# Dividing the input by its rms before the projection, and moving projection results and chain copies from VectorE to ScalarE

## The chip, the cores and the metric

The kernel runs on one core of a Trainium2 chip. A core has TensorE (PE in the profile, matmuls; PEld its weight loads), VectorE (DVE), ScalarE (ACT), GpSimd (POOL) and SyncE (SP, whose queue issues the DMAs here). The metric is the device time of one run in microseconds (us). Before the change it is 3194.62 us, the median of three runs from 3189.17 to 3198.58.

## The reference, cut to what matters

One layer of a hybrid decoder trunk over a prompt of 2048 tokens and 8 single-token samples, all in float32, width 1024. The part that the change touches:

```python
h = rmsnorm(x, norm_mix)                      # x / sqrt(mean(x*x)) * w, per token
p = h @ w_in                                  # 1024 -> 3980 columns, one projection for all groups
# group A: gated DeltaNet, chunks of 64 tokens
qkv = silu(causal_conv(p_a, 4 taps));  q, k = l2norm(q), l2norm(k)
v_new = u_i - w_i @ s                         # chunk by chunk, s carried from chunk to chunk
s = s * g_last + k_dec.T @ v_new
# group B: RWKV-7, the same carried state in another form
decay = exp(-exp(w0 + tanh(wd) @ w2)); a = sigmoid(a0 + ad @ a2)
# group C: HGRN2, chunks of 64
x = x + concat(y_a, y_b, y_c) @ w_out
x = x + (silu(h2 @ w_gate) * (h2 @ w_up)) @ w_down      # h2 = rmsnorm(x)
y = rmsnorm(x)
```

The rms of a token is one number per column of `p` in the kernel's transposed layout, so it can be applied to `x` ahead of the product or to `p` behind it.

## The kernel before, in words

Everything is kept transposed: features on the 128 partitions, tokens along the free axis. The tokens are cut into four quarters (`QS`): three of 512 and a last one of 520 (512 prompt tokens and the 8 samples), which is taken as two passes of 260 columns.

A large product is three matmuls for each of 8 slices of the contraction (`mm3`, L377 to L379): weight and input are split into a high and a low part, and high*high, high*low and low*high are added up in one PSUM bank. So one tile of the projection (128 output features by 512 tokens, tile `psp`) is 24 matmuls of 128x512. The pool `pg` has three banks for them. `proj` (L471) makes the 31 tiles of a quarter and multiplies each with the quarter's `rstd` on DVE (L482) on its way to the tile `p`, which a DMA then stores in DRAM (`s_p`). `split_x` (L409) makes the high part of the input on ACT (L417) and the low part on DVE (L418); `xs` has 8 buffers, one for each slice, so a quarter's first split waits until the quarter before has used that slice for the last time. `stats_x` (L426) makes `rstd`: squares on ACT, their sum on DVE, a matmul with ones, and Ln and Exp on ACT (`rsqs`, L290, with a table load at L285). It also makes the 12 columns `pba` of the projection (L447) and multiplies them with `rstd` (L452). For quarters 1 to 3 it runs at the sixth of the eight groups of tiles (`AT` = 5) of the quarter before.

From the stored `p` the mixers work, for each quarter three units of group A (`gdn`), three of B (`rwkv`) and two of C (`hgrn`). A unit of A or B has a first stage (convolution at L827 to L829, or token shift and decay, then triangular inverses) and a second one, a chain over 8 chunks. In each chunk stand three steps of small matmuls, `px`, `pv` and `pS`, with a result on DVE between any two of them: `X` (L900 or L1121), `Z` or `SA` (L906, L1128), and the next `Z` (L913, L1134). The second stages of one A unit and one B unit often run at the same time.

After the projections come, quarter by quarter, the output product (tile `pso`), and the FFN (`pfg`, `pfu`, `pd`); a quarter's end normalisation (`final`, tiles `pny` and `ry`) is done in steps within the next quarter's `out_proj`.

The program's order is made in two steps. `Driver` (L1460) takes turns: each turn advances all live units by one step and then emits as many large products as a rate for the quarter allows. The framework then sorts each engine's instructions by its own planning. Each engine runs its list strictly in that order, so an instruction that waits holds up all behind it on that engine; TensorE's list mixes large products with small matmuls of the mixers.

Of the kernel before, what the change touches and what calls it, by code (L numbers as in the profile page):

```python
# [13 lines left out]
AF = mybir.ActivationFunctionType  # L14
ALU = mybir.AluOpType
# [11 lines left out]
G = 512  # L27
# [3 lines left out]
QS = ((0, 512), (512, 512), (1024, 512), (1536, 520))  # L31
# [60 lines left out]
class Kern:  # L92
# [332 lines left out]

    def stats_x(self, q, load):  # L426

        nc = self.nc
        acc = self.new_acc(f"i{q}")
        if q == 0:  # L430
            nc.sync.dma_start(self.wba, self.io["wba"].rearrange("p (k j) -> p k j", j=32)[:, :, 0:12])
            nc.vector.tensor_tensor(self.wba, self.wba, self.parw("norm_mix")[:, :, None].to_broadcast([128, 8, 12]),
                                    ALU.mult)

        with ExitStack() if q else self.tc.issue_after(self.last.ins):
            for k in range(8):
                self.add_square(acc, load[k], self.cols(q), k == 0, f"i{q}", self.S if q else self.T)
        rstd = self.norm_stats(acc, self.cols(q), f"i{q}", q == 0)

        new = self.S if q else self.T  # L440
        p = new(f"pba{q}")
        for c0, cn in self.cols(q):
            cs = slice(c0, c0 + cn)
            ps = self.bank(f"psb{q}_{c0}")[:, :cn]
            for k in range(8):
                j = 32 * (k % 4)
                nc.tensor.matmul(ps[j:j + 12], lhsT=self.wba[:, k], rhs=load[k][:, cs], start=k < 4, stop=k > 3,  # L447
                                 tile_position=(0, j))
            nc.vector.tensor_copy(p[0:12, cs], ps[0:12])
            for j in (32, 64, 96):  # L450
                nc.vector.tensor_tensor(p[0:12, cs], p[0:12, cs], ps[j:j + 12], ALU.add)
            nc.vector.tensor_tensor(p[0:12, cs], p[0:12, cs], rstd[0:12, cs], ALU.mult)  # L452
        self.ba(q, p)
        return rstd

# [15 lines left out]
    def proj(self, qs, m, xs, rstd, w=None, stats=None, held=()):  # L471

        nc = self.nc
        w = w or held or self.load_w(self.io["w1"][m], ("in", m), qs[0])
        for q in qs:
            t0, n = QS[q]
            p = self.E(f"p{q}_{m}")
            for c0, cn in self.cols(q):
                ps = held[0] if held else self.gemm8(w, xs[q], c0, cn, f"psp{q}_{m}_{c0}")
                if q not in rstd:  # L480
                    rstd[q] = stats()
                nc.vector.tensor_tensor(p[:, c0:c0 + cn], ps, rstd[q][:, c0:c0 + cn], ALU.mult)  # L482

            if q < 3:
                nc.sync.dma_start(self.s_p[q + 1][m, :, 0:HALO], p[:, G - HALO:G])
            else:
                nc.scalar.activation(self.tail[:, m], p[:, G - HALO:G], AF.Copy)
                nc.scalar.activation(self.smp[:, m], p[:, G:G + NS], AF.Copy)
            self.mark = nc.sync.dma_start(self.s_p[q][m, :, HALO:], p[:, :n])
# [263 lines left out]
    def half(self, pair, h, other=False):  # L753

        return self.heads(pair[h], other)(h)
# [40 lines left out]
    def gdn(self, q, u):  # L796

        nc = self.nc
        t0 = QS[q][0]
        nm = f"g{q}{u}"  # L800
# [3 lines left out]
        def first():  # L804
# [18 lines left out]
            for which in (1, 0, 2):  # L823
                pt = self.slice_p(q, T_G + 4 * u + which, 3, f"p_{nm}")
                x = kq2[:, 1 - which] if which < 2 else self.T(f"cv_{nm}")
                wi = 4 * (3 * which + u)
                nc.vector.tensor_scalar(x, pt[:, 3:3 + G], self.par("conv", wi + 3), None, ALU.mult)  # L827
                for j in (2, 1, 0):
                    nc.vector.scalar_tensor_tensor(x, pt[:, j:j + G], self.par("conv", wi + j), x, ALU.mult, ALU.add)  # L829
                yield  # L830
                self.gate(x, x)
                if which < 2:
                    sq = self.T(f"sq_{nm}")
                    nc.scalar.activation(sq, x, AF.Square)
                    sums[which] = self.bsum(f"ss_{nm}", sq), sq
                    made = made or self.mm
                    yield
# [50 lines left out]
        def second():  # L888
            U, Q, kb3, vb3, kd, sg = (box[n] for n in ("U", "Q", "kb", "vb", "kd", "sg"))

            Z = [ch(self.T(f"Z{h}_{nm}")) for h in range(2)]
            st = self.state["g", u]
            for h in range(2):
                nc.vector.tensor_copy(half(Z, h)[:, 0], st[H[h]])
            for c in range(GC):
                px = self.ps(f"px_{nm}")[:, 0:64]
                for h in range(2):
                    nc.tensor.matmul(px[H[h]], lhsT=kb3[H[h], c], rhs=half(Z, h)[:, c], start=True, stop=True)
                X = self.X(f"X_{nm}")
                nc.vector.tensor_tensor(X, px, vb3[:, c], ALU.add)  # L900
                yield
                pv_ = self.ps(f"pv_{nm}")[:, 0:64]
                for h in range(2):
                    nc.tensor.matmul(pv_[H[1 - h]], lhsT=U[H[h], c], rhs=X[H[h]], start=True, stop=True)
                for h in range(2):
                    nc.vector.tensor_copy(half(Z, h, True)[:, c], pv_[H[1 - h]])  # L906
                yield
                pS = self.ps(f"pS_{nm}")[:, 0:64]
                for h in range(2):
                    nc.tensor.matmul(pS[H[h]], lhsT=kd[H[1 - h], c], rhs=half(Z, h, True)[:, c], start=True, stop=True)  # L910
                for h in range(2):
                    to = half(Z, h)[:, c + 1] if c + 1 < GC else st[H[h]]
                    nc.vector.scalar_tensor_tensor(to, half(Z, h)[:, c], sg[H[h], c:c + 1], pS[H[h]],  # L913
                                                   ALU.mult, ALU.add)
                yield
            yield NEXT
            po = self.ps(f"po_{nm}")
            for c in range(GC):
                for h in range(2):
                    nc.tensor.matmul(ch(po)[H[h], c], lhsT=Z[h][:, c], rhs=Q[h][:, c], start=True, stop=True)  # L920
            z = self.slice_p(q, T_G + 4 * u + 3, 0, f"z_{nm}")
            self.gated_norm(po, z, self.gnw2, nm, u, t0)
# [69 lines left out]
    def rwkv(self, q, u, lo):  # L992
# [7 lines left out]
        def first():  # L1000
# [4 lines left out]
            lw, cu = self.T(f"lw_{nm}"), self.T(f"cu_{nm}")  # L1005
            ps = self.ps(f"pw_{nm}")
            nc.tensor.matmul(ps, lhsT=self.w2a2[0:64, us], rhs=wa[0:64], start=True, stop=True)
            self.rwkv_decay(lw, ps, u)
            nc.vector.tensor_tensor_scan(cu, self.reset, lw, 0.0, ALU.mult, ALU.add)
            yield  # L1010

            f = self.sp.tile([128, GC], F32, tag="f", name=f"f_{nm}")
# [12 lines left out]
            nc.scalar.activation(e1, e1, AF.Exp)  # L1025
            nc.scalar.activation(e2, d, AF.Exp)
            nc.scalar.activation(d, d, AF.Exp, scale=-1.0)
            a = self.T(f"a_{nm}")
            ps = self.ps(f"paa_{nm}")
            nc.tensor.matmul(ps, lhsT=self.w2a2[64:128, us], rhs=wa[64:128], start=True, stop=True)  # L1030
            self.rwkv_rate(a, ps, u)
            yield
            k = self.shifted(q, T_R + 3 * u + 1, 3 + u, f"k{nm}")
            kr = self.TT(f"kr_{nm}")
            kk, r, t = kr[:, 0], kr[:, 1], self.T(f"t_{nm}")
# [74 lines left out]
        def second():  # L1110
# [5 lines left out]
            for c in range(GC):  # L1116
                px = self.ps(f"px_{nm}")[:, 0:64]
                for h in range(2):
                    nc.tensor.matmul(px[H[h]], lhsT=W[0][h][:, c], rhs=Z[h][:, c], start=True, stop=True)
                X = self.X(f"X_{nm}")  # L1120
                nc.vector.tensor_copy(X, px)  # L1121
                for h in range(2):
                    nc.vector.scalar_tensor_tensor(KV[H[h], c], half(Z, h)[:, c], f[H[h], c:c + 1], KV[H[h], c],
                                                   ALU.mult, ALU.add)
                yield
                pv_ = self.ps(f"pv_{nm}")[:, 0:64]
                self.pair(lambda p: pv_[p], lambda p: U[p, c], lambda p: X[p])
                nc.vector.tensor_copy(SA[:, c], pv_)  # L1128
                yield
                pS = self.ps(f"pS_{nm}")[:, 0:64]  # L1130
                self.pair(lambda p: pS[p], lambda p: bt[p, c], lambda p: SA[p, c])
                if c + 1 < GC:
                    for h in range(2):
                        nc.vector.tensor_tensor(half(Z, h)[:, c + 1], pS[H[h]], KV[H[h], c], ALU.add)  # L1134
                else:
                    nc.vector.tensor_tensor(st, pS, KV[:, c], ALU.add)
                yield
# [561 lines left out]
```

## Time and profile before

| | |
|---|---|
| median of three runs | 3194.62 us (3189.17 to 3198.58) |
| profiled execution | 3185.85 us, span 3184.1 us |
| PE busy | 3063.0 us (96%), 24812 matmuls |
| DVE busy | 2189.0 us (69%), 5424 instructions |
| ACT busy | 1196.6 us (38%), 2064 instructions |
| granted TensorE clock, mean | 0.985 of full speed |
| HBM traffic | 628.01 MB by DMA, 197 GB/s |

The busy shares are over the whole span. Three stretches differ: up to about 1014 us the projections and the mixers of the first quarters run together, from there to about 2640 us the FFNs and the remaining mixers, and behind that only large products of the last quarters. A matmul's duration in the profile overlaps the next one's, so what a matmul costs is read from start to start, not from its length.

### The profile page before, as it was taken

The page shows a single profiled execution, that of the slowest core. Times are in us where ns is not written, and L with a number is a line of the kernel's source. Part 1 is how long each engine was busy: PE and PEld are TensorE (multiplying, and loading weights), DVE is VectorE, ACT ScalarE, POOL GpSimd, SP SyncE. Part 2 cuts the span into 40 slices and gives each one's busy share as a digit, 9 for nine tenths or more (in the row PEclk, how much of TensorE's full clock was granted, in tenths as well). Part 3 has the DMA queues.
Part 4 walks back from the last instruction along what each step waited for, and adds up shares of the span by engine and source line. Part 5 has one row for each costly group of instructions (what it writes and reads, how often), then busy time and mean ns, then how long its engine had stood idle before and what let it go on. Part 6 is the DMA issues. An engine that isn't in the chain of part 4 may idle for free.

```text
span 3184.1 us, 62691 instructions
## 1 busy us (share of the span) xinstructions
PE 3063.0 (96%) x24812; PEld 2442.2 (77%) x24812; DVE 2189.0 (69%) x5424; ACT 1196.6 (38%) x2064; POOL 12.3 (0%) x41
## 2 busy tenths in 40 slices
PE   7999999999998999999989999999999999999998
PEld 5767767778897677677766777777777777999998
DVE  6783666677768888896978778868877653443334
ACT  5452243245324544543555334445433221221002
POOL 0000000000000000000000000000000000000000
PEclk9999999999999999999999999999999999999999
DMA  8877666657656766677764454557554465755552
GB/s 286 287 244 250 193 182 199 207 168 228 185 164 172 235 229 221 223 221 257 226 219 149 153 163 146 190 165 233 165 162 150 151 216 183 251 170 186 189 182 90
DMA packets 391971, 628.01 MB, mean 197 GB/s; under 512 B 172988, under 2 KB 177340, under 8 KB 391676
## 3 DMA queue, kind: packets, MB, share of 16 engines
q1 hardware_dynamic: 390588, 622.93, 61.4%
q8 instruction: 195, 3.19, 0.4%
q10 hardware_dynamic: 1088, 1.07, 0.1%
q14 instruction: 100, 0.82, 0.1%
HBM read 456.77 MB, written 167.14 MB: 196 GB/s over the span
## 4 chain that ended last, share of the span: by engine, by line
PE 68%; DVE 13%; DMA 11%; ACT 4%; SPq 2%; issue 2%; DVEq 0%; ACTq 0%
PE psp L377 5%; PE psp L379 5%; PE psp L378 5%; PE pfg L378 4%; PE pfg L377 4%; PE pfg L379 4%; PE pfu L377 4%; PE pfu L378 4%; PE pfu L379 4%; PE pd L377 4%; PE pd L379 4%; PE pd L378 4%; PE pso L377 1%; PE pso L378 1%; PE pso L379 1%
## 5 line engine op out<-in xcount | busy, mean ns | idle before, releaser
L377 PE MATMUL psp<-xs,w_in 128*128 128x512 f32 (+1 forms) x1240 | 448.7, 362 | 23.8 <-ACT w_in L332 9.7
L378 PE MATMUL psp<-xs,w_in 128*128 128x512 f32 (+1 forms) x1240 | 444.1, 358 | 0.3 <-DVE xs L418 0.3
L379 PE MATMUL psp<-xs,w_in 128*128 128x512 f32 (+1 forms) x1240 | 443.6, 359 | 0.0
L377 PEld LDWEIGHTS psp<-xs,w_in 128*128 128x128 f32 x1240 | 236.6, 191 | 67.9 <-ACT w_in L332 11.2
L379 PEld LDWEIGHTS psp<-xs,w_in 128*128 128x128 f32 x1240 | 236.0, 190 | 41.7 <-issue 4.5
L378 PEld LDWEIGHTS psp<-xs,w_in 128*128 128x128 f32 x1240 | 236.5, 191 | 35.4 <-issue 2.0
L606 DVE TENSOR_TENSOR x<-pd,x 128x512 f32<-128x512 f32 (+1 forms) x240 | 137.5, 582 | 104.0 <-PE pd L379 102.6
L377 PE MATMUL pfg<-xhs,w_wg 128*128 128x512 f32 x464 | 188.2, 406 | 7.3 <-ACT w_wg L332 4.8
L378 PE MATMUL pfg<-xhs,w_wg 128*128 128x512 f32 x464 | 188.8, 407 | 3.1 <-DVE xhs L564 3.1
L377 PE MATMUL pd<-u,w_wd 128*128 128x512 f32 x448 | 179.3, 409 | 10.4 <-DVE x L606 7.0
L379 PE MATMUL pfg<-xhs,w_wg 128*128 128x512 f32 x464 | 187.1, 403 | 0.1
L377 PE MATMUL pfu<-xhs,w_wu 128*128 128x512 f32 x464 | 186.5, 402 | 0.0
L378 PE MATMUL pfu<-xhs,w_wu 128*128 128x512 f32 x464 | 186.3, 402 | 0.0
L379 PE MATMUL pfu<-xhs,w_wu 128*128 128x512 f32 x464 | 185.0, 399 | 0.0
L378 PE MATMUL pd<-u,w_wd 128*128 128x512 f32 x448 | 178.9, 400 | 0.6 <-DVE u L363 0.6
L379 PE MATMUL pd<-u,w_wd 128*128 128x512 f32 x448 | 178.9, 400 | 0.0
L585 ACT ACTIVATE t<-t 128x512 f32<-128x512 f32 (+1 forms) x110 | 60.0, 546 | 281.2 <-DVE t L584 277.5
L285 ACT ACT_TABLE_LOAD x91 | 116.8, 1283 | 112.6 <-PE yv_r L275 18.9
L362 ACT ACTIVATE u<-t 128x512 fp32r<-128x512 f32 (+1 forms) x110 | 60.0, 545 | 216.7 <-DVE t L588 216.7
L482 DVE TENSOR_TENSOR p<-psp,ri 128x512 f32<-128x512 f32 (+1 forms) x155 | 89.8, 580 | 71.8 <-PE psp L379 70.5
L377 PE MATMUL pd<-u,hw_wd 128*128 128x260 f32 (+1 forms) x432 | 128.2, 307 | 3.9 <-ACT u L362 3.9
L378 PE MATMUL pd<-u,hw_wd 128*128 128x260 f32 (+1 forms) x432 | 131.3, 305 | 0.0
(648 smaller groups left out, 7318.8 us busy)
## 6 DMA issues: line engine op xcount, KB each, us to landing
w_in<-sw_in SPq DMA_DIRECT2D x186, 512.0 KB
w_wg<-sw_wg SPq DMA_DIRECT2D x72, 512.0 KB
w_wu<-sw_wu SPq DMA_DIRECT2D x72, 512.0 KB
w_wd<-sw_wd SPq DMA_DIRECT2D x68, 512.0 KB
sw_in<-w_in SPq DMA_DIRECT2D x62, 512.0 KB
s_p<-p SPq DMA_DIRECT2D x93, 256.0 KB
sw_wg<-w_wg SPq DMA_DIRECT2D x44, 512.0 KB
sw_wu<-w_wu SPq DMA_DIRECT2D x44, 512.0 KB
```

What stands on the lines that cost most here:

```text
L285: p = self.nc.scalar.preload_act_table_set("natural_log_exp_and_others")
L362: nc.scalar.activation(out[:, 0], src, AF.Copy)
L377: nc.tensor.matmul(ps, lhsT=hi[:, ws], rhs=xs[:, 0, xc], start=start, stop=False)
L378: nc.tensor.matmul(ps, lhsT=hi[:, ws], rhs=xs[:, 1, xc], start=False, stop=False)
L379: nc.tensor.matmul(ps, lhsT=lo[:, ws], rhs=xs[:, 0, xc], start=False, stop=stop)
L482: nc.vector.tensor_tensor(p[:, c0:c0 + cn], ps, rstd[q][:, c0:c0 + cn], ALU.mult)
L585: nc.scalar.activation(t, g, AF.Tanh, scale=0.5)
L606: nc.vector.tensor_tensor(x2[d][:, c0:c0 + cn], ps, x2[d][:, c0:c0 + cn], ALU.add)
```

## The change

- `stats_x` multiplies, for quarters 1 to 3, the eight input tiles `x` with `rstd` in place (8 instructions on DVE for each quarter), ahead of the small product L447 and of `split_x`. The multiplication of `pba` falls away for these quarters.
- `proj` then only copies its results for quarters 1 to 3, on ACT (new L486), where DVE multiplied before (L482). The first quarter stays as it was.
- The first tap of the convolution (L827) goes from DVE to ACT.
- In the chains, one of the two copies of `Z` in a unit of A (L906), and the copies `X` (L1121) and `SA` (L1128) in a unit of B go from DVE to ACT.
- In the first stage of `rwkv` the product and tanh for `a` stand beside those of the decay, ahead of the exponentials; one `yield` goes, so that a unit of B takes one turn less.

```diff
 stats_x:
         rstd = self.norm_stats(acc, self.cols(q), f"i{q}", q == 0)
+        if q:
+            for x in load:
+                nc.vector.tensor_tensor(x[:, :QS[q][1]], x[:, :QS[q][1]], rstd[:, :QS[q][1]], ALU.mult)
...
-            nc.vector.tensor_tensor(p[0:12, cs], p[0:12, cs], rstd[0:12, cs], ALU.mult)
+            if not q:
+                nc.vector.tensor_tensor(p[0:12, cs], p[0:12, cs], rstd[0:12, cs], ALU.mult)
 proj:
-                if q not in rstd:
-                    rstd[q] = stats()
-                nc.vector.tensor_tensor(p[:, c0:c0 + cn], ps, rstd[q][:, c0:c0 + cn], ALU.mult)
+                if q:
+                    nc.scalar.activation(p[:, c0:c0 + cn], ps, AF.Copy)
+                else:
...
 gdn, first:
-                nc.vector.tensor_scalar(x, pt[:, 3:3 + G], self.par("conv", wi + 3), None, ALU.mult)
+                nc.scalar.activation(x, pt[:, 3:3 + G], AF.Copy, scale=self.par("conv", wi + 3))
 gdn, second:
-                for h in range(2):
-                    nc.vector.tensor_copy(half(Z, h, True)[:, c], pv_[H[1 - h]])
+                nc.scalar.activation(half(Z, 0, True)[:, c], pv_[H[1]], AF.Copy)
+                nc.vector.tensor_copy(half(Z, 1, True)[:, c], pv_[H[0]])
 rwkv, first:
+            a = self.T(f"a_{nm}")
+            psa = self.ps(f"paa_{nm}")
+            nc.tensor.matmul(psa, lhsT=self.w2a2[64:128, us], rhs=wa[64:128], start=True, stop=True)
             self.rwkv_decay(lw, ps, u)
             nc.vector.tensor_tensor_scan(cu, self.reset, lw, 0.0, ALU.mult, ALU.add)
+            self.rwkv_rate(a, psa, u)
             yield
...
-            a = self.T(f"a_{nm}")
...
-            self.rwkv_rate(a, ps, u)
-            yield
 rwkv, second:
-                nc.vector.tensor_copy(X, px)
+                nc.scalar.activation(X, px, AF.Copy)
...
-                nc.vector.tensor_copy(SA[:, c], pv_)
+                nc.scalar.activation(SA[:, c], pv_, AF.Copy)
```

The planning answers to the new lists with another order on every engine. Three places are shown; in the names, `p1_29` is tile 29 of quarter 1, and `g22` or `r22` unit 2 of group A or B in quarter 2.

On ACT, at the start of the output product of quarter 1, stands the Ln `ry0` that releases a bank of `pg`. Before, five table loads stand from the first row to it:

```order
L285 ACT_TABLE_LOAD
L793 ACT_TABLE_LOAD
L793 ACTIVATE th_17249<-cols_gs1_17240 128x8
L296 ACT_TABLE_LOAD
L296 ACTIVATE sq_g22_16896<-ss_g22_16898,par_t_90 128x512
L793 ACT_TABLE_LOAD
L793 ACTIVATE th_17307<-cols_gs1_17240 128x8
L285 ACT_TABLE_LOAD
L296 ACTIVATE ry0_0_19858<-pny0_0_19863,par_t_90 128x512
```

Now the same Ln has other work ahead of it, on ACT at the same place:

```order
L285 ACT_TABLE_LOAD
L296 ACTIVATE osq_g21_17937<-oss_g21_17942,par_t_90 128x512
L801 ACT_TABLE_LOAD
L801 ACTIVATE th_18197<-cols_gs2_17958 128x8
L285 ACT_TABLE_LOAD
L296 ACTIVATE ry0_0_20158<-pny0_0_20163,par_t_90 128x512
```

Three table loads are left in this piece.

On PE, in the FFN of quarter 1, the chains of `g22` and `r22` run together. Before, a step of each stands between two large matmuls:

```order
L378 MATMUL pd1_2_22431<-u1_9_22239,w_wd_2_1_1_22427 128x512
L910 MATMUL pS_g22_19921<-Z0_g22_18358,kd_g22_17648 64x64
L910 MATMUL pS_g22_19921<-Z1_g22_18359,kd_g22_17648 64x64
L259 MATMUL pv_r22_20097<-X_r22_19970,N_r22_18283 64x64 x2
L379 MATMUL pd1_2_22431<-u1_9_22239,w_wd_2_1_1_22427 128x512
```

Now, on PE in the same FFN, they come apart:

```order
L378 MATMUL pfu1_5_21621<-xhs1_0_20614,w_wu_5_1_21591 128x512
L259 MATMUL pv_r22_19770<-X_r22_19703,N_r22_18067 64x64 x2
L379 MATMUL pfu1_5_21621<-xhs1_0_20614,w_wu_5_1_21591 128x512
L377 MATMUL pfu1_5_21621<-xhs1_1_20617,w_wu_5_1_21591 128x512
L378 MATMUL pfu1_5_21621<-xhs1_1_20617,w_wu_5_1_21591 128x512
L912 MATMUL pv_g22_19654<-X_g22_19621,N_g22_17178 64x64 x2
L379 MATMUL pfu1_5_21621<-xhs1_1_20617,w_wu_5_1_21591 128x512
```

The step of B, which follows a copy on ACT, and the step of A, which follows an instruction on DVE, now interrupt the large product twice.

On ACT, where quarter 1 of the projection ends and quarter 2 is split, the list was before:

```order
L417 ACTIVATE xs2_5_6274<-raw_x24_3789,par_t_90 128x512
L272 ACTIVATE hi_kss_r02_4266<-kr_r02_4204 128x512
L417 ACTIVATE xs2_6_6277<-raw_x26_3792,par_t_90 128x512
L417 ACTIVATE xs2_7_6280<-raw_x26_3792,par_t_90 128x512
L285 ACT_TABLE_LOAD
```

Now the last two results of quarter 1 and chain copies are on ACT at this place:

```order
L417 ACTIVATE xs2_6_6394<-raw_x26_3836,par_t_90 128x512
L486 ACTIVATE p1_29_6265<-psp1_29_6215 128x512
L486 ACTIVATE p1_30_6269<-psp1_30_6216 128x512
L417 ACTIVATE xs2_7_6397<-raw_x26_3836,par_t_90 128x512
L1128 ACTIVATE X_r01_4566<-px_r01_4563 128x64
L913 ACTIVATE Z0_g02_4410<-pv_g02_4471 64x64
```

The two results stand behind seven of the eight splits and ahead of the eighth.

## Rows read from the trace of the kernel before

**Rows 1.** The page's first line: busy time, share of the span, instructions.
```profile
PE 3063.0 (96%) x24812; PEld 2442.2 (77%) x24812; DVE 2189.0 (69%) x5424; ACT 1196.6 (38%) x2064; POOL 12.3 (0%) x41
```
**Rows 2.** Windows: stretch, length, then each engine's busy time (instructions), clock, DMA.
```profile
256.00:1014.00 758.00, 739.04 (x6979) 592.20 (x6978) 508.10 (x1375) 267.23 (x488) 1.66 (x8) 0.99 0.64 194
1014.00:2640.00 1626.00, 1572.41 (x12492) 1177.96 (x12492) 1272.39 (x3159) 715.60 (x1198) 3.16 (x6) 0.99 0.60 194
```
**Rows 3.** Waits of PE, 256 to 1014 us: sum, times, longest.
```profile
PE po_r L1142 <- DVE Z_r L1134: 2.7, 1, 2.7
...
PE pS_r L259 <- DVE SA_r L1128: 0.2, 1, 0.2
```
**Rows 4.** Waits of PE, 1014 to 2640 us.
```profile
PE pd L377 <- DVE x L606: 7.0, 6, 1.9
PE pso L377 <- ACT ry L296: 6.8, 1, 6.8
...
PE ptv_g L739 <- DVE cv_g L841: 0.5, 1, 0.5
PE ss_g L274 <- ACT hi_ss_g L272: 0.4, 1, 0.4
```
**Rows 5.** Groups by line and shape, DVE: count, busy, mean ns; idle before.
```profile
L482 DVE TENSOR_TENSOR p<-psp,ri 128x512 f32<-128x512 f32 x93 | 63.6, 685 | 53.8 <-PE psp L379 53.1
L906 DVE COPY Z_g<-pv_g 64x64 f32<-64x64 f32 x192 | 42.7, 222 | 42.9 <-PE pv_g L904 21.5 <-PE pS_r L259 14.2 <-PE pl_h L1237 2.3
L482 DVE TENSOR_TENSOR p<-psp,ri 128x260 f32<-128x260 f32 x62 | 26.2, 423 | 18.0 <-PE psp L379 17.3
L827 DVE TENSOR_SCALAR kq_g<-p_g,par_t 128x512 f32<-128x512 f32 x24 | 10.8, 475 | 2.0 <-DMA p_g<-s_p 2.0
```
**Rows 6.** The same view of ACT: the nearest operations to the new ones.
```profile
L285 ACT ACT_TABLE_LOAD x91 | 116.8, 1283 | 112.6 <-PE yv_r L275 18.9 <-PE oss_g L275 16.4 <-PE pnf L512 16.0
L712 ACT ACTIVATE N_r<-pj_r 32x256 f32<-32x256 f32 x48 | 18.0, 374 | 10.6 <-PE pj_r L710 10.0
L948 ACT ACTIVATE kr<-pkr,derived 128x512 f32<-128x512 f32 x12 | 8.6, 715 | 23.6 <-PE px_g L898 23.6
L1144 ACT ACTIVATE y_r<-po_r 128x512 f32<-128x512 f32 x12 | 7.2, 598 | 47.4 <-PE po_r L1142 47.1
```
**Rows 7.** Timeline of PE, two chain steps of two units together: start, length.
```profile
306.83 0.39 PE L378 MATMUL psp<-xs,w_in 128*128 128x512 f32 x1
...
307.28 0.40 PE L377 MATMUL psp<-xs,w_in 128*128 128x512 f32 x1
307.61 0.33 PE L898 MATMUL px_g<-Z_g,kb_g 64*64 64x64 f32 x4
...
308.33 0.39 PE L379 MATMUL psp<-xs,w_in 128*128 128x512 f32 x1
```
**Rows 8.** Timeline of PE, one chain step alone.
```profile
1613.88 0.40 PE L377 MATMUL pso<-mxs,w_o 128*128 128x512 f32 x1
1614.21 0.33 PE L904 MATMUL pv_g<-X_g,N_g 64*64 64x64 f32 x4
...
1614.81 0.39 PE L379 MATMUL pso<-mxs,w_o 128*128 128x512 f32 x1
```
**Rows 9.** Timeline of ACT around the Ln of `ry`.
```profile
1616.38 1.28 ACT L285 ACT_TABLE_LOAD   x1 [0.50 <-PE ss_g L275]
...
1624.01 0.69 ACT L296 ACTIVATE ry<-pny,par_t 128x512 f32<-128x512 f32 x1
```
**Rows 10.** Timeline of PE at the same place.
```profile
1624.74 0.79 PE L377 MATMUL pso<-mxs,w_o 128*128 128x512 f32 x1 [6.76 <-ACT ry L296]
...
1629.18 0.42 PE L378 MATMUL pso<-mxs,w_o 128*128 128x512 f32 x1
```
**Rows 11.** Window behind that wait; the column behind POOL is the granted clock.
```profile
1624.70:1629.20 4.50, 4.46 (x11) 3.49 (x12) 0.77 (x2) 4.44 (x6) 0.00 (x0) 0.50 0.12 50
```
**Rows 12.** Waits of ACT, 256 to 1014 us.
```profile
ACT xs L417 <- PE psp L379: 31.4, 7, 28.3
```

More of the change, by code (lines that the diff above doesn't have):

```diff
@@ L479, in proj @@
                 ps = held[0] if held else self.gemm8(w, xs[q], c0, cn, f"psp{q}_{m}_{c0}")
-                if q not in rstd:
-                    rstd[q] = stats()
-                nc.vector.tensor_tensor(p[:, c0:c0 + cn], ps, rstd[q][:, c0:c0 + cn], ALU.mult)
+                if q:
+                    nc.scalar.activation(p[:, c0:c0 + cn], ps, AF.Copy)
+                else:
+                    if q not in rstd:
+                        rstd[q] = stats()
+                    nc.vector.tensor_tensor(p[:, c0:c0 + cn], ps, rstd[q][:, c0:c0 + cn], ALU.mult)
             if q < 3:
@@ L1027, in first @@
             nc.scalar.activation(d, d, AF.Exp, scale=-1.0)
-            a = self.T(f"a_{nm}")
-            ps = self.ps(f"paa_{nm}")
-            nc.tensor.matmul(ps, lhsT=self.w2a2[64:128, us], rhs=wa[64:128], start=True, stop=True)
-            self.rwkv_rate(a, ps, u)
-            yield
             k = self.shifted(q, T_R + 3 * u + 1, 3 + u, f"k{nm}")
```

## The prediction

> **What bounds the kernel now.** I read the page's first line, then the windows by stage, then what PE waited for in each, and last the timelines at single places. PE is busy 96% of the span, DVE 69%, ACT 38% [rows 1]. In the stretch of the projections PE is busy 739.0 of 758 us, in the stretch of the FFNs with the remaining mixers 1572.4 of 1626 [rows 2]. So all that any other engine can give back is PE's idle time: 19 us in the first stretch and 54 in the second; the rest of the 121 us lies at the start, before 256 us, and behind 2640 us, where the change does little. The share of DVE in the second stretch (1272 of 1626 us, 78%) looks high, but PE's waits are the measure. In the first stretch nine of them, 8.2 us in sum, are put down to DVE, from 2.7 us to 0.2 [rows 3]; in the second twelve with 20.6 us (the first 7.0, the last 0.5) and eleven with 23.7 us to ACT (6.8 to 0.4) [rows 4]. The product of a quarter's tile is never seen waiting for its bank because of the multiplication in L482.
>
> **What moves, and what it costs where.** Off DVE go 62 results of 512 columns at 0.685 us (quarters 1 and 2), 62 of 260 columns at 0.423, 36 first taps at 0.475, and 288 copies of 64 columns (96 of `Z`, 96 `X`, 96 `SA`) at 0.222 [rows 5]: 42.5 + 26.2 + 17.1 + 63.9 = 150 us. On it come 24 multiplications of the input, at 0.685 like the other 512-column products: 16. Net -133 us, 2189 to about 2056. ACT takes 62 copies at 0.598 (the PSUM copy L1144), 62 of 260 columns at about 0.374 (L712, 256 columns), 36 scaled copies at 0.715 (L948) and the 288 small ones [rows 6]. These have no row; the line through L712 and L1144 gives 0.21 us at 64 columns, and L712 is the upper bound. I take 0.21: 37 + 23 + 26 + 60 = 146 us. In the order of ACT the table loads fall from 195 to 192, since tanh for `a` now precedes the exponentials; at 1.283 us each that is 4 us. Net +142 us, 1197 to about 1340, or 42%. Neither sum touches the end by itself: both engines stay far below PE.
>
> The Trainium skill (ScalarE: Activation LUTs, section What ACT_TABLE_LOAD costs) gives an activation with immediate scale and bias 186 ns plus 0.833 ns per element. By it a 64-column copy would take an estimated 239 ns, slower than DVE's 222 in the trace; over 288 copies that is 5 us of chain, which the chain's distance to its next user hides. At 512 columns the same rule gives 613 ns, close to the measured 598.
>
> Dividing the input ahead adds a wait: the small product L447 and the split of the next quarter now stand behind `rstd`. It is made at the sixth of eight groups, eleven tiles of 24 matmuls ahead of the quarter's end, and a large matmul starts every 0.225 us (two in 0.45, from 306.83 to 307.28) [rows 7]: 59 us of cover for 5.5 us of multiplications on DVE. Cost 0; without that cover it would be 5.5 us for each of three quarters. The stores of `p` only change the engine that they wait for.
>
> **Four terms reach PE.** First, the order. A chain step alone between large matmuls costs 1613.88 to 1614.81, 0.93 us, less the 0.45 of its two large neighbours: 0.48 [rows 8]. Two steps of two units in one place cost 307.28 to 308.33, 1.05 less 0.45: 0.60 [rows 7]. So each time that two steps come apart costs 0.36 us. In the order of PE the places with nothing but chain steps rise from 199 to 241, since units of A and B now follow different engines and come ready at different moments; mixed places fall from 504 to 498 and lose 29 steps, of 0.12 us each at the second step's price. That is 42 x 0.36 = 15, less 29 x 0.12 = 3 and 6 x 0.36 = 2: about +10. Bounds: 0, if steps in one place cost as much as apart, and 15.
>
> Second, the wait of 6.76 us at the start of quarter 1's output product: PE wants the bank that `ry` holds, and ACT needs from 1616.38 to 1624.70 for five table loads and what lies between [rows 9, 10]. In the new order three loads stand there: 3 x 1.28, two Ln at 0.69, one small tanh at 0.2, in sum 5.4 us from the first load's release. PE has some 2.5 us of small work of its own between that release and the wait (an estimate: `pny` and the sums at 0.23 for each 128x512 matmul, the transposes and the inverse's small ones). A wait of 3 us is left: -4. Behind the old wait the granted clock is 0.50, the 1.2 GHz level [rows 11], and ten large matmuls take 4.44 us instead of 2.25 [rows 10]. Since PE still waits, I count half of these 2.2 us: -1. Together -5; bounds 0 and -9.
>
> Third, DVE is relieved. The waits on DVE, 8.2 + 20.6 = 29 us, belong mostly to work that doesn't move (the FFN's sums L606, the splits); the moved copies cause little (`SA` 0.2 us [rows 3]). With 6% less on the engine I take a quarter of them: -7. Bounds 0 and -29.
>
> Fourth, ACT has 12% more to do in these stretches. Without `ry`, 17 us of PE's waits in the second stretch are put down to it; twice the proportion gives +4. Bounds 0 and +17, if all of them doubled.
>
> Sum: +10 - 5 - 7 + 4 = +2 us on 3185.85, the profiled execution's own time. That execution is 8.8 us faster than the median of the three runs, so in the runs' terms 3194.6 + 2, about 3196: no change that can be told, since 0.3%, some 9.6 us, is about what a measurement of this kernel can tell.
>
> **Rivals.** (a) Slower: ACT's strict order holds results back. At a quarter's end the split waits up to 28.3 us for PE [rows 12]. A result of the projection queued behind such a wait keeps its bank; with three banks PE runs at most two tiles on, 2 x 24 x 0.225 = 11 us, and then stands for 17. The two ends of quarters 1 and 2 would cost 34 us: 3229. It decides once PE's waits at L377 for L486 pass 10 us. For it: seven splits, each waiting for PE, stand close together with results and chain copies. Against: the order puts both last results ahead of the eighth split, and PE's own product paces both. The Trainium skill (TensorE: Matmul & The Clock Gate, section Architectural detail) calls ScalarE strictly first in, first out; that is the rule by which this would happen. Chance 0.16.
>
> (b) Slower by the order alone: the steps come apart at the full 15 us, the relief is nothing, `ry` stays as it was: 3194.6 + 15 + 4 = 3214. For it: the count of places is certain, since PE's order is fixed. Against: twelve places of 8 matmuls or one odd one do not all cost the same. Chance 0.10.
>
> (c) Faster: most DVE waits go, and with them some stretches at half clock. Of the 29 us, 20 go, `ry` loses all of 9, the order costs 8: about -21, plus the +4 of ACT: 3178. For it: DVE is the fullest engine beside PE in the second stretch, and its late results cascade into ACT's (the FFN's `u`). Against: the waits are single, short, and on work that stays. Chance 0.35.
>
> Forecast, within 0.3%: 0.39; its own range is 3185 to 3204.
>
> **How the numbers follow.** The time is the forecast's, 3196. The low end takes (c) with another 10 us, 3166; the high end reaches almost to (a), 3226, and leaves about 0.08 above and 0.1 below. Faster by over 0.3% is (c), 0.35; within it 0.39; slower is (a) and (b), 0.26.
>
> **What the profile will show.** DVE near 2056 us, ACT near 1340. The 64-column copies on ACT near 0.21 us and no PE wait over 1 us for them. No L377 wait for L486. Between two large matmuls, single chain steps more often. The wait for `ry` near 3 us. The idle time of PE outside 256 to 2640 us as before. I am wrong if PE's idle time in these stretches changes by more than 15 us, or if PE's busy time rises by more than 15.

## The result and the profile after

The change made the kernel slower: 3211.06 us, the median of five runs (3209.46 to 3221.97), against 3193.31 of the kernel before, measured beside it (five runs, 3189.17 to 3198.58). The ratio is 1.0062, with a 95% interval from 1.0041 to 1.0083. The time lies inside the predicted range, but not where the likeliest case put it: forecast were 3196 and no change that can be told. The profiled execution has a span of 3209.1 us, 25.0 more than before; the one profiled before (3185.85 us) was 7.5 us faster than the median of its kernel, the one after is the median itself, so some 7 of the 25 us are the spread between executions. Nearest came the rival "slower by the order alone" with 3214, but the experiments do not bear its mechanism out.

The page's first line of the kernel after, to be read beside [rows 1]:

```profile
PE 3095.1 (96%) x24812; PEld 2456.4 (77%) x24812; DVE 2084.0 (65%) x4996; ACT 1328.0 (41%) x2509; POOL 12.3 (0%) x41
```

PE's idle time is the span less its busy time. It fell from 121.1 to 114.0 us. PE's busy time rose by 32.1. So all that was lost, and more, lies where PE counts as busy with the same 24812 matmuls. The mean granted clock went from 0.985 to 0.980. As a clock c over a span s means 2(1-c)s at the lower level of 1.2 GHz, that is some 96 us before and 128 after. Of this time PE is busy 71.6 us before and 91.2 after; half of it is what the level costs, since large matmuls start every 0.43 us there and every 0.23 us at full clock: 35.8 and 45.6 us. So some 10 of the 32 us are lost at the lower level, and 22 are not.

The windows by stage of the kernel after, answering [rows 2] (stretch, length, busy time of PE, PEld, DVE, ACT, POOL, granted clock, DMA share, GB/s):

```profile
256.00:1014.00 758.00, 743.08 (x6915) 582.35 (x6914) 451.45 (x1196) 353.50 (x721) 1.65 (x8) 0.99 0.63 191
1014.00:2640.00 1626.00, 1574.61 (x12424) 1182.35 (x12423) 1225.98 (x2923) 758.48 (x1402) 3.15 (x6) 0.98 0.61 193
```

The groups by line that took over the moved work, of the kernel after (they answer [rows 5, 6]):

```profile
L486 ACT ACTIVATE p<-psp 128x512 f32<-128x512 f32 x62 | 36.8, 594 | 82.7 <-PE psp L379 81.3 <-DMA inD<-s_ur 0.9
L486 ACT ACTIVATE p<-psp 128x260 f32<-128x260 f32 x62 | 23.8, 385 | 58.0 <-PE psp L379 57.7
L1135 ACT ACTIVATE SA_r<-pv_r 128x64 f32<-128x64 f32 x96 | 21.2, 221 | 58.5 <-PE pv_r L259 53.7 <-PE pk_r L1073 3.5 <-PE pl_h L1244 0.5
L913 ACT ACTIVATE Z_g<-pv_g 64x64 f32<-64x64 f32 x96 | 21.0, 218 | 64.1 <-PE pv_g L912 42.5 <-PE pv_r L259 19.8
```

The durations came as estimated: 218 to 221 ns for 64 columns where 0.21 was taken, against 216 to 222 for the same copies on DVE before. The Trainium skill (ScalarE: Activation LUTs, section What ACT_TABLE_LOAD costs) gave an estimated 239; the measurement decides.

Two groups of waits of PE in the kernel after, first from 256 to 1014 us, then from 1014 to 2640 (they answer [rows 3, 4]):

```profile
PE pni L520 <- DVE sqli L516: 2.1, 1, 2.1
...
PE pS_r L259 <- ACT SA_r L1135: 0.9, 1, 0.9
```
```profile
PE pl_h L1244 <- DVE att_h L1247: 7.4, 3, 4.0
PE pd L377 <- DVE x L614: 5.9, 3, 4.7
...
PE pso L377 <- ACT ry L296: 1.6, 1, 1.6
```

The wait for `ry` fell from 6.8 to 1.6 us. No wait at L377 for a result of L486 is in either list, nor in the rest of the trace.

**Where the time went.** The large matmuls of the projection, the first 3720, come in the same order in all kernels here and can be counted through (from 0); behind them the order of the FFN's differs, but by the later counts used here each kernel has run the same ones. From the 422nd to the 554th, in the projection of the first quarter where the statistics of the next are made, the kernel before needs 47.5 us (from 142.7 to 190.2), the kernel after 68.3. The same stretch around the second statistics (1197th to 1328th) takes 51.2 and 61.7 us, around the third (1911th to 2073rd) 60.0 and 68.8: in sum 40 us more, with 303, 278 and 426 small matmuls among them against 250, 348 and 302 before, so a part of the first and third is only small work done earlier. Of the first stretch's 20.8 us 15.5 lie between the 478th and the 510th large matmul (15.4 us before, 30.9 after); in the second stretch the piece from the 1197th to the 1225th takes 13.3 us before and 28.0 after. At the 3720th (1022.1 us before) the kernel after lags 45 us and has done 563 small matmuls more; at the 7589th (2300.1 us) it lags 64, with 614 more done. The 18 us in between are lost behind the last division, and no experiment names their cause. By the 8664th (2644.0 us), when both have done all small work of the mixers, 37 of these have come back and 27 stay.

The timeline of PE in the kernel before, at the first of these places: `psb` runs right behind the first sum `pni`, and large matmuls follow.

```profile
167.28 0.50 PE L511 MATMUL pni<-sqhi,ones 128*128 128x512 f32 x1 [0.70 <-DVE sqhi L507]
167.71 1.91 PE L447 MATMUL psb<-raw_x,wba 128*12 128x512 f32 x16
169.55 0.50 PE L377 MATMUL psp<-xs,w_in 128*128 128x512 f32 x1
```

The same place in the kernel after, PE's timeline:

```profile
163.83 0.40 PE L379 MATMUL psp<-xs,w_in 128*128 128x512 f32 x1
164.16 0.33 PE L912 MATMUL pv_g<-X_g,N_g 64*64 64x64 f32 x4
...
166.64 0.50 PE L519 MATMUL pni<-sqhi,ones 128*128 128x512 f32 x1 [0.15 <-DVE sqhi L515]
168.03 0.33 PE L918 MATMUL pS_g<-Z_g,kd_g 64*64 64x64 f32 x4 [0.90 <-DVE Z_g L914]
...
172.20 0.77 PE L520 MATMUL pni<-sqli,ones 128*128 128x512 f32 x1
172.90 0.48 PE L906 MATMUL px_g<-Z_g,kb_g 64*64 64x64 f32 x4
175.26 0.48 PE L912 MATMUL pv_g<-X_g,N_g 64*64 64x64 f32 x4 [1.88 <-DVE X_g L908]
177.49 0.48 PE L928 MATMUL po_g<-Q_g,Z_g 128*64 128x64 f32 x2 [1.75 <-ACT Z_g L913]
...
178.87 1.88 PE L451 MATMUL psb<-raw_x,wba 128*12 128x512 f32 x2
180.68 0.79 PE L377 MATMUL psp<-xs,w_in 128*128 128x512 f32 x1
```

From the start of one large matmul at 163.83 to that of the next at 180.68 are 16.85 us (5.6 before, from 163.92 to 169.55). The large ones stand in PE's list behind the first two of `psb`, and `psb` stands behind the division. What it waits for is on ACT and DVE, in the same kernel:

```profile
173.00 1.28 ACT L285 ACT_TABLE_LOAD   x1
174.29 0.69 ACT L296 ACTIVATE ri<-pni,par_t 128x512 f32<-128x512 f32 x1
175.00 1.28 ACT L801 ACT_TABLE_LOAD   x1
...
177.23 0.21 ACT L913 ACTIVATE Z_g<-pv_g 64x64 f32<-64x64 f32 x1
177.46 0.63 ACT L299 ACTIVATE ri<-ri 128x512 f32<-128x512 f32 x1
```
```profile
178.12 0.69 DVE L442 TENSOR_TENSOR raw_x<-raw_x,ri 128x512 f32<-128x512 f32 x1 [0.22 <-ACT ri L299]
178.73 0.20 DVE L693 TENSOR_TENSOR inU_r<-inU_r,inT_r 64x56 f32<-64x56 f32 x1
178.86 4.29 DVE L442 TENSOR_TENSOR raw_x<-raw_x,ri 128x512 f32<-128x512 f32 x7
```

The chain from the sum over Ln, a foreign table load and Exp to the first multiplication ends at 178.81, and `psb` starts at 178.87. In the meantime PE has only chain steps left, whose results stand behind the same tables: `Z_g` at 177.23 comes 1.5 us after its product ended, behind a table load, a tanh and a copy. This is how the moved chain copies show up as waits; the Trainium skill (TensorE: Matmul & The Clock Gate, section Architectural detail) calls ScalarE strictly first in, first out, and this place agrees, though on a chain copy and not on the projection's results. At the second place (413.81 to 428.53) again no large matmul runs for 14.7 us; there the first multiplication is done at 424.17, and other small work keeps `psb` until 426.71. The third place is different: between the same two large matmuls the kernel before needs 12.3 us, and the kernel after 11.7. The 8.8 us of the third stretch lie elsewhere in it, beside 124 small matmuls more.

The windows up to the fall of the clock at the first place and behind it, in the kernel after:

```profile
163.80:170.30 6.50, 3.98 (x35) 2.25 (x35) 6.42 (x16) 2.02 (x6) 0.00 (x0) 1.00 0.64 172
170.30:183.90 13.60, 9.94 (x55) 6.16 (x51) 12.49 (x37) 7.86 (x13) 0.20 (x2) 0.50 0.31 96
```

PE was busy 3.98 of 6.5 us, with no single wait over 0.9, and then ran 13.6 us at 1.2 GHz, the first large matmuls among them.

### The profile page after: what moved, and what is told of

It reads as the page before. It is cut to its first block, busy times and chain, and to the rows that moved or that the text cites. A ratio compares the mean times of both kernels' runs of the same rounds, so it can differ in the third digit from the quotient of the medians.

```text
span 3209.1 us, 62806 instructions
## 1 busy us (share of the span) xinstructions
PE 3095.1 (96%) x24812; PEld 2456.4 (77%) x24812; DVE 2084.0 (65%) x4996; ACT 1328.0 (41%) x2509; POOL 12.3 (0%) x41
## 5 line engine op out<-in xcount | busy, mean ns | idle before, releaser
L377 PE MATMUL psp<-xs,w_in 128*128 128x512 f32 (+1 forms) x1240 | 448.4, 362 | 19.3 <-ACT xs L417 8.4
L377 PEld LDWEIGHTS psp<-xs,w_in 128*128 128x128 f32 x1240 | 235.5, 190 | 67.1 <-issue 10.7
L377 PE MATMUL pd<-u,w_wd 128*128 128x512 f32 x424 | 172.1, 414 | 10.2 <-DVE x L614 5.9
L377 PE MATMUL pfg<-xhs,w_wg 128*128 128x512 f32 x432 | 175.9, 407 | 1.2 <-ACT w_wg L332 1.2
L378 PE MATMUL pfg<-xhs,w_wg 128*128 128x512 f32 x432 | 176.1, 408 | 0.1
L379 PE MATMUL pfg<-xhs,w_wg 128*128 128x512 f32 x432 | 175.2, 406 | 0.3 <-DVE w_wg L333 0.3
L377 PE MATMUL pfu<-xhs,w_wu 128*128 128x512 f32 x432 | 174.3, 403 | 0.0
L379 PE MATMUL pfu<-xhs,w_wu 128*128 128x512 f32 x432 | 174.0, 403 | 0.0
L378 PE MATMUL pfu<-xhs,w_wu 128*128 128x512 f32 x432 | 173.1, 401 | 0.0
L378 PE MATMUL pd<-u,w_wd 128*128 128x512 f32 x424 | 171.8, 406 | 0.8 <-DVE u L363 0.7
L379 PE MATMUL pd<-u,w_wd 128*128 128x512 f32 x424 | 170.9, 404 | 0.3 <-DVE w_wd L333 0.3
L377 PE MATMUL pfg<-xhs,hw_wg 128*128 128x260 f32 (+1 forms) x448 | 138.4, 310 | 5.0 <-ACT xhs L571 4.4
L378 PE MATMUL pd<-u,hw_wd 128*128 128x260 f32 (+1 forms) x456 | 139.8, 308 | 0.0
L378 PE MATMUL pfg<-xhs,hw_wg 128*128 128x260 f32 (+1 forms) x448 | 138.8, 310 | 0.9 <-DVE xhs L572 0.9
```

The lines of the kernel that those rows point to most:

```text
L377: nc.tensor.matmul(ps, lhsT=hi[:, ws], rhs=xs[:, 0, xc], start=start, stop=False)
L378: nc.tensor.matmul(ps, lhsT=hi[:, ws], rhs=xs[:, 1, xc], start=False, stop=False)
L379: nc.tensor.matmul(ps, lhsT=lo[:, ws], rhs=xs[:, 0, xc], start=False, stop=stop)
```

## The experiments

Each kernel was timed in five rounds beside the kernel before (medians 3190.7, 3191.6 and 3190.2 us in the three groups). The columns: places is how often PE's list passes from large matmuls to small ones; idle is the span less PE's busy time; the last column is the time of the three stretches above, between the same large matmuls.

| kernel | us | ratio to before (95%) | places | idle | clock | stretches |
|---|---|---|---|---|---|---|
| before | 3190 to 3193 | 1 | 703 | 121.1 | 0.985 | 47.5, 51.2, 60.0 |
| after | 3211.1 | 1.0062 (1.0041 to 1.0083) | 739 | 114.0 | 0.980 | 68.3, 61.7, 68.8 |
| e1 division alone | 3183.4 | 0.9977 (0.9964 to 0.9990) | 698 | 112.6 | 0.981 | 57.1, 57.9, 65.9 |
| e2 chain copies alone | 3209.0 | 1.0049 (1.0032 to 1.0065) | 725 | 115.3 | 0.978 | 48.4, 43.9, 54.2 |
| e3 `rwkv` move alone | 3200.6 | 1.0028 (1.0015 to 1.0040) | 663 | 132.7 | 0.979 | 47.9, 50.6, 54.5 |
| e4 after, `psb` first | 3191.5 | 0.9998 (0.9986 to 1.0011) | 690 | 113.9 | 0.984 | 51.2, 43.5, 55.5 |
| e5 after, no chain copies | 3219.3 | 1.0086 (1.0065 to 1.0106) | 664 | 134.4 | 0.976 | 67.3, 56.9, 68.1 |
| e6 after, no `rwkv` move | 3217.6 | 1.0087 (1.0068 to 1.0107) | 745 | 114.3 | 0.980 | 60.6, 55.1, 68.1 |
| e7 after, no division | 3217.2 | 1.0079 (1.0060 to 1.0099) | 713 | 125.1 | 0.975 | 52.9, 53.0, 54.7 |
| e8 first tap alone | 3195.9 | 1.0013 (1.0001 to 1.0024) | 704 | 124.9 | 0.980 | 51.5, 46.6, 59.0 |
| e9 before, rates down | 3197.3 | 1.0020 (1.0008 to 1.0033) | 671 | 126.5 | 0.980 | 47.8, 52.4, 57.9 |
| e10 before, rates up | 3175.2 | 0.9953 (0.9938 to 0.9968) | 689 | 111.0 | 0.980 | 48.3, 52.4, 58.5 |
| e11 after, rates down | 3217.3 | 1.0082 (1.0064 to 1.0099) | 706 | 118.4 | 0.977 | 70.2, 65.2, 71.4 |
| e12 after, rates up | 3205.8 | 1.0049 (1.0034 to 1.0063) | 729 | 115.1 | 0.980 | 67.0, 61.8, 68.9 |

**One part alone, and one thing undone.**

e1, the division:

```diff
+        if q:
+            for x in load:
+                nc.vector.tensor_tensor(x[:, :QS[q][1]], x[:, :QS[q][1]], rstd[:, :QS[q][1]], ALU.mult)
...
+                if q:
+                    nc.scalar.activation(p[:, c0:c0 + cn], ps, AF.Copy)
```

> The kernel before with one part of the change: the input divided ahead of the projection for quarters 1 to 3, and the results copied by ACT. Theory A (the division is at fault: the 12-column product psb now waits for eight multiplications, comes apart on PE, and small work stands in clumps behind it, followed by stretches at the 1.2 GHz level): PE's busy time rises by 10 to 15 us, the time to about 3203, +10. Theory B (chain steps that come apart, 0.36 us for each place with nothing but chain steps; here 200 places against 199): no change, 3193. Theory C (ACT's heavier load): 124 results more on ACT, none of them in a chain; at most +2.

e2, the chain copies (so also for `Z` and `SA`):

```diff
-                nc.vector.tensor_copy(X, px)
+                nc.scalar.activation(X, px, AF.Copy)
```

> The kernel before with one part: a copy of Z, and the copies X and SA, go to ACT. Theory A: nothing of the division is in it, PE's busy time stays within 5 us, time 3193. Theory B: 220 places with nothing but chain steps against 199, 21 x 0.36: +8, 3201. Theory C: ACT's load with chain copies behind 1.3 us table loads makes PE wait: idle time of PE up by 5 or more.

e3, the move in `rwkv`:

```diff
             self.rwkv_decay(lw, ps, u)
             nc.vector.tensor_tensor_scan(cu, self.reset, lw, 0.0, ALU.mult, ALU.add)
+            self.rwkv_rate(a, psa, u)
             yield
...
-            self.rwkv_rate(a, ps, u)
-            yield
```

> The kernel before with one part: the product and tanh for a beside those of the decay, one turn less for a unit of B. Theory A: no change, 3193. Theory B: 172 places with nothing but chain steps against 199: -10, 3183. A third theory D (any change re-sorts the small work, and where it falls in clumps of over 5 us without a large matmul decides, whatever the part is): some us either way, with the sum of such clumps (57 us before, 112 after) telling the sign.

e4, the change with `psb` ahead of the division:

```diff
-        if q:
-            for x in load:
-                nc.vector.tensor_tensor(x[:, :QS[q][1]], x[:, :QS[q][1]], rstd[:, :QS[q][1]], ALU.mult)
         p = new(f"pba{q}")
...
-            if not q:
-                nc.vector.tensor_tensor(p[0:12, cs], p[0:12, cs], rstd[0:12, cs], ALU.mult)
+            nc.vector.tensor_tensor(p[0:12, cs], p[0:12, cs], rstd[0:12, cs], ALU.mult)
         self.ba(q, p)
+        if q:
+            for x in load:
+                nc.vector.tensor_tensor(x[:, :QS[q][1]], x[:, :QS[q][1]], rstd[:, :QS[q][1]], ALU.mult)
```

> The changed kernel with the 12-column product psb taken from the undivided input, ahead of the division, and pba multiplied with rstd as before; all else as in the change. Theory A: psb stands in 4 places again in place of 9, PE's busy time falls by 8 to 15 us, time about 3200. Theory B: 197 places with nothing but chain steps in place of 241: -16, 3195. Theory C: nothing changes, 3211.

e4 gives back the 20 us. PE's timeline at the first place, of e4:

```profile
165.56 0.50 PE L518 MATMUL pni<-sqhi,ones 128*128 128x512 f32 x1 [0.15 <-DVE sqhi L514]
165.99 1.91 PE L448 MATMUL psb<-raw_x,wba 128*12 128x512 f32 x16
167.83 0.51 PE L377 MATMUL psp<-xs,w_in 128*128 128x512 f32 x1
```

Ahead of this place PE's list is as in the kernel after, instruction by instruction; now large matmuls run while `rstd` is made. From the 478th to the 510th large matmul e4 takes 15.6 us, as e7 does, which has the same list there and no division; the kernel after takes 30.9. The window from 162 to 190 us, of the kernel before, of the kernel after and of e4:

```profile
162.00:190.00 28.00, 27.13 (x165) 19.01 (x163) 23.62 (x58) 21.46 (x32) 0.30 (x3) 1.00 0.83 265
```
```profile
162.00:190.00 28.00, 21.82 (x123) 12.57 (x120) 23.51 (x63) 13.42 (x24) 0.20 (x2) 0.76 0.45 135
```
```profile
162.00:190.00 28.00, 27.01 (x163) 18.90 (x163) 27.06 (x63) 15.44 (x29) 0.20 (x2) 1.00 0.66 198
```

e4 lies 3.5 us below theory B's 3195 and 8.5 below theory A's 3200, so it does not part them well, but B fails elsewhere: e3, with the fewest places, is 10 us slower where B has 10 faster, and e2 loses 18 where B has 8. C fails with e4, since ACT's load is the same there (busy 1325.4 us against 1328.0), and in e2 PE's idle time falls to 115.3 where C has it rise. A names the place of the loss, but has none for e2 and e3, and fails on the sign of e1: the three stretches are longer by 9.6, 6.7 and 5.9 us, and yet the kernel is 7 us faster. What e1 wins outside is in its idle time (112.6) and 40 us less work on DVE, and was not taken apart further. D's sign, the sum of the pieces of over 5 us without a large matmul (from the end of one to the start of the next: 50 us before, 98 after, and 75, 88, 80 and 58 in e1 to e4), is right for e2 and e3 and, against the kernel after, for e4, and wrong for e1.

e2 and e3 lose in another place. The window of e2 in which the last mixers' steps stand together:

```profile
2558.00:2600.00 42.00, 28.14 (x391) 21.80 (x390) 35.45 (x102) 15.64 (x34) 0.52 (x1) 0.59 0.09 28
```

PE's timeline in it, of e2:

```profile
2558.26 0.40 PE L379 MATMUL pd<-u,w_wd 128*128 128x512 f32 x1
...
2574.34 1.34 PE L1142 MATMUL po_r<-W_r,Z_r 128*64 128x64 f32 x20 [4.12 <-ACT osq_g L296]
...
2582.71 1.61 PE L1237 MATMUL pl_h<-lv_h 64*64 64x64 f32 x32 [3.26 <-DVE att_h L1240]
...
2600.26 0.50 PE L377 MATMUL pd<-u,hw_wd 128*128 128x512 f32 x1
```

For 42 us no large matmul stands between the chains, PE is busy two thirds of it at a clock of 0.59. In e3 such a stretch has 41 us, in e7 57; in the kernel before the longest near there has 7. It does not take a part of the change: e9, the kernel before at other rates, has two shorter ones there, of 21 and 16 us, and e8 one of 20. Behind the 7589th large matmul e2 falls from 2 us ahead of the kernel before to 22 behind it, e3 from 3 behind to 15.

**Theory E and the control.** E makes the time of three sums: PE's work at full clock (busy time less half of what runs at 1.2 GHz: 3027.2 before, 3049.5 after), the half lost at 1.2 GHz, and the idle time. e5 puts these back:

```diff
-                nc.scalar.activation(X, px, AF.Copy)
+                nc.vector.tensor_copy(X, px)
```

> The changed kernel with the chain's copies Z, X and SA back on DVE; all else as in the change. Theory E (three sums of PE make the time: work at full clock, which grows by some 0.3 us for each place where small work stands between two large matmuls; time at the 1.2 GHz level, of which half is lost; idle time): places fall from 739 to 664, below the 703 of before, so work at full clock falls by 22 us against the change's 3049.5 to about 3020 or less, and the time to about 3183. Theory D (only clumps and the clock decide, places say nothing): work at full clock stays within 8 us of the change's, time anywhere from 3190 to 3211.

e6 puts `rwkv_rate` back behind the exponentials:

```diff
-            self.rwkv_rate(a, psa, u)
             yield
...
+            self.rwkv_rate(a, ps, u)
+            yield
```

> The changed kernel with the product and tanh for a back behind the exponentials, and the turn given back. Theory E: 745 places against 739 of the change: work at full clock 3049 to 3052, time about 3207 with the half clock of the other runs. Theory D: work at full clock does not follow the places; by the move alone, which made the kernel before 10 us slower, taking it back should give 10 us: 3201.

e7 undoes the division:

```diff
-                if q:
-                    nc.scalar.activation(p[:, c0:c0 + cn], ps, AF.Copy)
...
+                nc.vector.tensor_tensor(p[:, c0:c0 + cn], ps, rstd[q][:, c0:c0 + cn], ALU.mult)
```

> The changed kernel with the multiplication by rstd back behind the product, on DVE, and nothing divided ahead. Theory E: 713 places against 739: work at full clock 3049.5 - 8 = about 3041 or, with psb in 4 places again, 3035; time about 3198. Theory D: no relation to places; by the division alone, which made the kernel before 7 us faster, taking it back should cost 7: 3218.

e8 has the tap alone:

```diff
-                nc.vector.tensor_scalar(x, pt[:, 3:3 + G], self.par("conv", wi + 3), None, ALU.mult)
+                nc.scalar.activation(x, pt[:, 3:3 + G], AF.Copy, scale=self.par("conv", wi + 3))
```

> The kernel before with one part: the first tap of the convolution on ACT. A control for what a new order does by itself, since the part is 36 instructions of 0.5 us that no chain waits for. Theory E: 704 places against 703: work at full clock 3027, time 3191 within the 8 us that half clock and idle time spread over. Theory D: any re-sorting moves the time by about 10 us either way.

In time, E misses e5 by 36 us, e6 by 11 and e7 by 19, and fits e8; D is right on e7 and e8, and 8 and 17 us too low on e5 and e6. The work at full clock came out as 3022.0 in e5, where D has it stay, and 3049.8 in e6, near E's figures, but 3023.2 in e7 and 3016.3 in e8, 12 to 18 us and 11 us below them. And e5, with the fewest places of the changed kernels, has the highest median of all: its clock (0.976) and idle time (134.4) take back what it saves. The number of places is no predictor of the time. The parts do not add up either: alone they make -7, +18, +10 and +4, in sum 25 where the change costs 18 (e8's +4 is at the edge of what can be told), but taking any one of three out of the change makes it no faster: the medians are 6 to 8 us higher, though the intervals of the ratios overlap that of the change. e7 weighs most: without the division its three stretches are as short as in the kernel before, and it is 25 us slower than that kernel all the same, with a piece of 57 us without a large matmul near 2500 us. So the wait of `psb` is not the whole of the loss. Where a part goes, another order comes.

**How much is the order.** e9 to e12 change nothing but the rates of large products for each turn:

```diff
-RATES = (12.25, 14.25, 15.25, 19.25)
+RATES = (12.0, 14.0, 15.0, 19.0)
```

and (12.5, 14.5, 15.5, 19.5) for "up".

> The kernel before with nothing of the change, but with the rates of large products for each turn (RATES) some 1.5% lower: 12.0, 14.0, 15.0, 19.0 in place of 12.25, 14.25, 15.25, 19.25. It draws another order from the same parts. Theory D (the order as a whole makes the difference, not the parts): this kernel lies up to 25 us above the kernel before, 3191 to 3216, though nothing is moved between engines. Theory P (the parts of the change themselves cost time): within 5 us of the kernel before, 3187 to 3197.

> The same with the rates some 2% higher: 12.5, 14.5, 15.5, 19.5. Theory D: 3191 to 3216. Theory P: 3187 to 3197.

> The changed kernel with the rates 12.0, 14.0, 15.0, 19.0. Places between large matmuls fall from 739 to 706, those of chain steps alone from 241 to 188. Theory D: anywhere from 3190 to 3220, overlapping what the kernel before gives at the same rates. Theory P: within 5 us of the change's 3211, and 15 to 25 us above the kernel before at the same rates.

> The changed kernel with the rates 12.5, 14.5, 15.5, 19.5; 729 places, 228 of chain steps alone. Theory D: anywhere from 3190 to 3220, overlapping what the kernel before gives at the same rates. Theory P: within 5 us of 3211, and 15 to 25 us above the kernel before at the same rates.

Both theories lose a half. The order alone moves the kernel before by 22 us (3175 to 3197), so P's 5 us are wrong, and D has e10 at 3191 or more. But the changed kernel does not overlap with it, as D has it: at the rates of the kernel, down and up it is 18, 20 and 31 us slower, where P has 15 to 25. Its three stretches are long at each rate (67.0 to 70.2 us for the first, against 47.5 to 48.3). These are not three fresh orders, though: e12's list on PE is that of the kernel after for the first 11104 of 24812 matmuls (1370 us), and e11's up to the 988th, which takes in the first place. All six kernels in which `psb` waits for the division, with four different orders ahead of the first place, have a first stretch of 57 to 70 us, the eight others of 47.5 to 53; the second and third part likewise (55 to 65 us against 44 to 53, 66 to 71 against 54 to 60).

What is shown: the change costs 18 to 31 us at three rates, and with `psb` ahead of the division, at the rate of the kernel, those 20 us are back. Not tried is that step at the other two rates, so what of e4's 20 us is a kinder order is open; the three stretches take 48.6 us less in e4 (150.2 against 198.8 in sum), and in the first two, with 16 and 22 small matmuls fewer of some 300, 17 and 18; the third has 208 fewer. That `psb`'s wait costs some 15 us at the first place is shown (from the 478th to the 510th large matmul, with 93 small ones against 74 in e4), and that it costs about as much at the second, where the kernel after has 212 small ones against 176. That it makes the 18 us by which the whole kernel is slower is not shown, since e1 has the wait and is faster, and e7 has none and is slower. The fastest kernel is e10, the kernel before at higher rates, 0.9953 of it; e1 beats both kernels too, 0.9977. The two together were not run.

## Why the prediction was right and wrong

- **The waits, -5 - 7 + 4 = -8: the sum is right by luck.** PE's idle time fell by 7.1 us, 6.2 of them from 256 to 2640 us. The wait for `ry` fell from 6.76 to 1.62, by 5.1 where 4 was said. But the relief of DVE (-7) did not come: the waits put down to DVE rose in these stretches from 29.6 to 40.1 us, with `att_h` at 7.4 among them. ACT's extra work (+4) did not show: its waits without `ry` fell from 21.5 to 18.6. What closes the sum are the waits put down to DMA, 12.9 us before and 4.8 after, which the prediction has not.
- **Rival (c), most DVE waits go: did not come,** by the same numbers.
- **Rival (a), the projection's results held back on ACT: did not come.** PE has no wait for L486.
- **Engines.** ACT 1328 against about 1340, right. DVE 2084 against about 2056: the groups that changed fell by 134 us in their summed lengths, but the busy time by only 105, since instructions of DVE that follow each other closely overlap (at 178.12 one of 0.69 us, the next at 178.73), and a sum of lengths counts the overlap twice. All lengths on DVE add up to 2403.0 us before and 2269.0 after, the busy time to 2189.0 and 2084.0.
- **The order, +10 for chain steps that come apart: the price did not hold.** e2 and e3 miss it by 10 and 20 us, e3 on the other side; the count says little where clock and idle time move by more.
- **The division at cost 0, with 59 us of cover, and 5.5 us for each quarter without it: this is the step that failed.** The cover was counted as the large matmuls that remain until the splits need the divided input. But `psb` needs it at once, and PE takes its list strictly in order: the same large matmuls stand behind `psb` and cannot cover it. And what is exposed is not the 5.5 us of multiplications (PE waits for one of them only) but the whole chain from the sum over Ln, a foreign table load and Exp, and half the clock behind it: at the first place 16.85 us without a large matmul where the kernel before has 5.6, and 15 us more in the stretch around it, where 5.5 was the worst case; at the second place it is about as much, with more small work in it, and at the third nothing can be told.
- **The sign that would show it** was named: PE's busy time rising by more than 15. It rose by 32. Matmuls at half clock, and small ones that run without large ones beside them, count as busy. Some 10 of the 32 us are the lower clock (45.6 us lost there against 35.8); how much of the other 22 is small work without large matmuls beside it was not measured.
- **The time itself.** 3196 is 15 us too low. It lies within the range because the range was made wide for other reasons, the rivals (a) and (c). The low end, (c) less 10 us, is 3168 by its own numbers and not 3166; nothing hangs on it.

## What to carry to other kernels

When a step is moved ahead of a product, look at which is its first reader in the list of the engine that bounds the kernel, not at the last; on an engine that works in order, what stands behind that reader is no cover. Take small side products from the data as it is, and scale their small result. And where a planner sorts the whole program, compare a change at two or three settings that redraw the order, and look whether they do redraw it: here the order alone moves one kernel by 22 us, and one of the settings left the first 1370 us as they were.

## What the hardware showed

The granted clock fell to 0.50, the 1.2 GHz level, at 170.3 us although PE never waited longer than 0.9 us in one piece in the 6.5 us before; it was busy 3.98 of them, with small matmuls. The lower level then lasted 13.6 us, into the large matmuls. The Trainium skill (TensorE: Matmul & The Clock Gate, section A second HAM failure mode: psum-queue depth-cycling) tells of a kernel where frequent short idles between groups of matmuls make the clock change back and forth; this trace has such short idles ahead of the fall too, though PE waits in them for results of DVE and ACT. A copy of 64 columns out of PSUM takes the same on ACT (0.218 to 0.221 us) as on DVE (0.216 to 0.222), so moving such copies frees DVE's time and by its length costs the chain nothing; it costs what stands ahead on ACT, 1.5 us for `Z_g` at 175.74.
